# A two-part transformer on one core: the end of the expert stage re-ordered, its next pools opened earlier, and the state-space decays made a first job

## The chip, the cores and the metric

The kernel runs on 1 core of one Trainium2 chip, in one launch. The metric is the device time of that core in microseconds (us), the median of a few runs; smaller is better. The engines named below are PE (TensorE, matrix products), DVE (VectorE), ACT (ScalarE), POOL (GpSimd) and SP (SyncE, which issues most DMAs). Each works through its instructions in the order in which the program issued them.

## What is computed

512 tokens of width 1024, in fp32. Two layers run first, each of four steps; a forgetting attention, a gated MLP, an HGRN mixer and another gated MLP follow. Of a layer, this is what the change touches, in short form:

```python
x = x + merged @ w_out[i]            # the mixer; one of its four branches is bidir_ssd
x = x + expert_choice_moe(rms_norm(x, g_moe[i]), w_router[i], w_exp_gate[i], w_exp_up[i], w_exp_down[i])
ple_gate = sigmoid(rms_norm(x, g_ple[i]) @ w_ple_gate[i])
x = x + ple_gate * (p[i] @ w_ple[i])

def expert_choice_moe(h, w_router, w_gate_e, w_up_e, w_down_e):   # 16 experts, 64 tokens each
    affinity = softmax(h @ w_router)
    top_aff, idx = top_k(swapaxes(affinity, 1, 2), cap)
    xe = h[idx]
    hid = silu(xe @ w_gate_e) * (xe @ w_up_e)
    return zeros_like(h).at[idx].add((hid @ w_down_e) * top_aff)

def ssd_chunked(x, dt, a, bm, cm):                                # one direction, chunks of 128
    acs = cumsum(dt * a)                                          # within a chunk
    decay_in = exp(where(causal, acs[l] - acs[s], -inf))
    y_diag = ((cm @ bm.T) * decay_in) @ (x * dt)                  # + a state carried from chunk to chunk
```

`bidir_ssd` adds a forward and a backward pass of this over 4 heads.

## The kernel before

**Layout.** Activations stand feature-major: `x` is 8 tiles ("chunks") of 128 features x 512 tokens. Dense products split each fp32 weight into a rounded part (`ph`, a cast on ACT) and a rest (`pl`, a subtraction on DVE or POOL), and each activation chunk into two parts (both called `ach`): high part h on ACT, low part l on DVE. Each chunk then takes three 128x512 products. Expert weights are used whole, as the moving operand against 64 gathered rows.

**Expert stage** (`moe`). The 16 experts run as 8 pairs, p = 0 to 7. `gate(p)`, `up(p)` and `down(p)` each read 8 loads of 1 MB (4 per expert) and make 64 products. The program's loop over p issues: `turn` (transposes of the hidden rows), for odd p the four `gather`s of the next four experts' rows, `gate(p+1)`, for even p the `scatters` of finished pairs into `x` and `returns` (the one-hot products that bring rows back), `up(p+1)`, `down(p)`. Loads go to a ring of tiles in rotation: a main ring of 11 (`xraw`), one beside it (`xraw2`) and the shared 2 (`raw`). A load can be issued by SP only when the tile that it overwrites has been read. The first loads also borrow three tiles (`xraw3`).

**End of the stage.** After `up(7)` the main ring is closed, the pools of the next stage (`nxt`: its `ach` tiles) are opened, and a ring of 5 + 1 (`X.last`, `ring2`) with the shared 2 is opened. Then `ple_early` computes the embedding product p @ w_ple whole: a 1 MB load, two DMAs of pT, 6 casts on ACT and 6 subtractions on DVE (tiles `t2k`), and 48 products in 8 banks named `po`, each copied by ACT to `pw`. `down(6)` follows, and `down(7)` is made in two halves of output features (`half`): after half 0 all chunks get the older pairs, then chunks 0 to 3 the last pair; after half 1 chunks 4 to 7. Each `scatter(j)` sums into a bank `sm` (there are 2), DVE adds it to `x[j]` (`add_x`), and `nxt.chunk(j)` then issues for the next stage's norm: h (ACT), l (DVE), the square (ACT) and its addition (POOL or DVE). `nxt.prime(1)` loads and splits the first piece of `w_ple_gate`, at chunk 6.

**State-space branch** (`ssm`). It begins with `dt_proj`, softplus and cumulative sums (`col`, `dtv`, and `lrow`, written to memory to be read back broadcast), then convolutions (`taps`), per chunk states, and per head: `rows` (two tiles `M` of decays), `weights` (their sum, weighted by dt and multiplied by the scores `G`) and `outputs` (products into `po`). The branch is one of four jobs that the mixer's planner places beside the dense projections; it holds a cost for each instruction and a clock for each engine, and sets the order of all engines' programs when the kernel is built. Every instruction is recorded on line 196, so the trace is read by tile names.

## Time and profile before

| | |
|---|---|
| median of 3 runs | 3551.6 us (3550.32 to 3556.86) |
| the profiled execution | 3555.33 us, of which the span is 3553.5 us |
| PE busy | 3308.3 us, 93% of the span |
| DVE, ACT, POOL busy | 1708.9, 1103.9, 295.6 us |
| expert stage of layer 0, layer 1 | about 571 to 1091 us, about 1680 to 2199 us |
| mean granted PE clock | 0.977 of full speed |

The trace is one execution, its times in us from the start of the span. Launch and end, 1.83 us, lie outside the span. The clock column of a window is what the throttle granted to PE: the two levels are 1.2 and 2.4 GHz, so 1.00 means 2.4 GHz throughout, and a number between is a mix of the two. Idle time in square brackets stands ahead of the instruction in whose row it is, with what ended it.

### The profile page before, as it was taken

What the parts mean: (1) busy time and instruction counts of PE and PEld (TensorE: products, weight loads), DVE (VectorE), ACT (ScalarE), POOL (GpSimd) and SP (SyncE); (2) the same over time, 40 slices, a digit from 0 to 9 for tenths busy, and PEclk for the clock granted to TensorE, in tenths of its full rate; (3) what the DMA queues carried; (4) which work ended last, traced back from release to release, by engine and by line L of the source; (5) the groups of instructions that cost most, each with busy time, mean ns of one, the idle gap of its engine ahead of it and who ended that gap; (6) DMA issues with size and microseconds to landing.
All of it is one profiled execution on the core that took longest, in us unless ns stands there. A gap on an engine that the chain in (4) does not pass through costs nothing.

```text
span 3553.5 us, 41092 instructions
## 1 busy us (share of the span) xinstructions
PE 3308.3 (93%) x16658; PEld 2345.6 (66%) x16658; DVE 1708.9 (48%) x2914; ACT 1103.9 (31%) x1770; POOL 295.6 (8%) x176
## 2 busy tenths in 40 slices
PE   7999878998988999989999988999999999999998
PEld 6787665433336777766434434777888888878887
DVE  4565863011116546774211113654666567677555
ACT  3444322000014344322100003454434344334333
POOL 0001221000001000232000000311100000000000
PEclk9999989999999999999999999999999999999999
DMA  5242325999993332233999994222233232222222
GB/s 174 77 128 66 101 92 233 416 420 420 420 366 93 102 96 85 78 95 133 392 420 420 420 411 174 91 78 91 66 103 97 93 99 73 73 69 95 95 97 81
DMA packets 264893, 633.53 MB, mean 178 GB/s; under 512 B 20136, under 2 KB 192680, under 8 KB 215296
## 3 DMA queue, kind: packets, MB, share of 16 engines
q1 hardware_dynamic: 249136, 614.58, 46.4%
q10 hardware_dynamic: 15568, 16.32, 1.5%
q8 instruction: 131, 2.15, 0.3%
q14 instruction: 58, 0.48, 0.0%
HBM read 618.15 MB, written 4.31 MB: 175 GB/s over the span
## 4 chain that ended last, share of the span: by engine, by line
PE 42%; DMA 9%; DVE 4%; ACT 1%; issue 0%; SPq 0%; DVEq 0%; ACTq 0%
PE mm L196 36%; DMA xraw<-in_w_exp_down_dram 3%; DMA xraw<-in_w_exp_gate_dram 2%; PE po L196 2%; DMA xraw<-in_w_exp_up_dram 2%; PE sm L196 1%; PE t L196 1%; PE s L196 1%; PE a L196 1%; DVE x L196 1%; DVE pl L196 1%; DVE ach L196 1%; DMA raw<-in_w_exp_up_dram 1%; DMA raw<-in_w_exp_gate_dram 1%; DVE w L196 0%
## 5 line engine op out<-in xcount | busy, mean ns | idle before, releaser
L196 PE MATMUL mm<-ach,ph 128*128 128x512 f32 x5504 | 1748.1, 399 | 80.6 <-DVE w L196 45.7
L196 PEld LDWEIGHTS mm<-ach,ph 128*128 128x128 f32 x5504 | 1025.2, 190 | 324.8 <-issue 73.2
L196 PE MATMUL mm<-ach,pl 128*128 128x512 f32 x2752 | 1083.5, 394 | 0.5 <-DVE pl L196 0.5
L196 PEld LDWEIGHTS mm<-ach,pl 128*128 128x128 f32 x2752 | 523.3, 190 | 114.2 <-DVE pl L196 1.7
L196 PE MATMUL mm<-xraw,t2k 128*64 128x512 f32 x1776 | 461.1, 601 | 28.2 <-DMA xraw<-in_w_exp_gate_dram 21.2
L196 ACT CAST ph<-raw 128x1024 fp32r<-128x1024 f32 (+1 forms) x366 | 373.6, 1029 | 305.9 <-PE mm L196 258.9
L196 DVE TENSOR_TENSOR pl<-raw,ph 128x1024 fp32r<-128x1024 f32 (+1 forms) x317 | 389.2, 1231 | 99.8 <-ACT ph L196 97.6
L196 PEld LDWEIGHTS mm<-xraw,t2k 128*64 128x64 f32 x1776 | 146.7, 138 | 281.4 <-issue 225.9
L196 PE MATMUL mm<-xraw,hT 128*64 128x512 f32 x848 | 218.8, 599 | 26.6 <-DMA xraw<-in_w_exp_down_dram 26.6
L196 POOL TENSOR_TENSOR pl<-raw,ph 128x1024 fp32r<-128x1024 f32 x49 | 120.4, 2457 | 774.5 <-ACT ph L196 689.9
L196 DVE TENSOR_TENSOR sg<-sg,mm 128x512 f32<-128x512 f32 x32 | 22.0, 688 | 310.1 <-PE mm L196 310.1
L196 PEld LDWEIGHTS mm<-xraw,hT 128*64 128x64 f32 x848 | 68.5, 137 | 153.8 <-issue 106.4
L196 ACT ACTIVATE w<-w 128x512 f32<-128x512 f32 x130 | 80.2, 629 | 285.4 <-DVE w L196 275.0
L196 ACT ACTIVATE yy<-mm,ac 128x512 fp32r<-128x512 f32 x32 | 22.0, 687 | 419.8 <-PE mm L196 419.8
L196 DVE SCALAR_TENSOR_TENSOR yy<-mm,ac,yy 128x512 fp32r<-128x512 f32 x32 | 24.0, 751 | 248.7 <-ACT yy L196 247.7
L196 DVE SCALAR_TENSOR_TENSOR y<-u,small,y 128x512 f32<-128x512 f32 x176 | 131.8, 749 | 3.1
L196 PE MATMUL mm<-raw,t2k 128*64 128x512 f32 x272 | 124.1, 608 | 2.6 <-DMA raw<-in_w_exp_gate_dram 2.6
L196 DVE TENSOR_TENSOR x<-x,sm 128x512 f32<-128x512 f32 x80 | 54.2, 685 | 137.4 <-PE sm L196 137.4
L196 POOL TENSOR_TENSOR w<-w,w 128x512 f32<-128x512 f32 x64 | 96.1, 1513 | 272.0 <-DVE w L196 262.4
L196 DVE TENSOR_TENSOR w<-mm,R 128x512 f32<-128x512 f32 x92 | 63.0, 686 | 111.7 <-PE mm L196 104.6
L196 ACT ACTIVATE sg<-mm 128x512 f32<-128x512 f32 x32 | 19.1, 597 | 304.1 <-PE mm L196 304.1
L196 DVE TENSOR_TENSOR x<-x,mm 128x512 f32<-128x512 f32 x80 | 54.4, 684 | 122.1 <-PE mm L196 122.1
(306 smaller groups left out, 3370.0 us busy)
## 6 DMA issues: line engine op xcount, KB each, us to landing
xraw<-in_w_exp_gate_dram SPq DMA_DIRECT2D x112, 1024.0 KB, 19.9
xraw<-in_w_exp_up_dram SPq DMA_DIRECT2D x110, 1024.0 KB, 19.9
xraw<-in_w_exp_down_dram SPq DMA_DIRECT2D x106, 1024.0 KB, 19.8
raw<-in_ffn_w_up_dram SPq DMA_DIRECT2D x44, 1024.0 KB, 5.0
raw<-in_w_branch_gate_dram SPq DMA_DIRECT2D x32, 1024.0 KB, 5.3
raw<-in_w_in_dram SPq DMA_DIRECT2D x22, 1024.0 KB, 5.4
raw<-in_w_exp_down_dram SPq DMA_DIRECT2D x22, 1024.0 KB, 19.9
raw<-in_w_exp_up_dram SPq DMA_DIRECT2D x18, 1024.0 KB, 19.9
```

The source lines that it names most:

```text
L196: r = g(*a, **kw)
```

## The change

It has two parts.

**Expert stage.** (1) The 16 tiles of normalised rows (`t2k`) move to a pool of their own on the other side of memory, which is closed after the last gathers; gathered rows `xe` get 3 tiles and a shared one. (2) The rings: `ring2` is 2 instead of 1 and the last ring 6 instead of 5, and a queue of slots takes the place of the counting; `down(6)` and `down(7)` no longer use the shared `raw` tiles. (3) Closing the main ring, opening the next stage's pools and the last ring come at p = 5, after `gate(6)`. (4) `ple_early` is a generator and goes in pieces: the load of `w_ple` and the two DMAs of pT before `up(6)`; casts and subtractions after `up(6)`; 24 products after `down(5)`; 12 after `gate(7)` with its scatters and returns; 12 after `up(7)`. (5) `nxt.fetch()` issues the first two loads of `w_ple_gate` before half 1's loads, and `nxt.prime(2)` splits two pieces before half 1 is weighed. (6) The low part l and the addition of the square are issued after the next chunk's addition (`behind`), and in half 1 the odd chunks sum into a `po` bank.

**State-space branch.** `decays` (the beginning of `ssm`) is a job of its own ahead of all four, plus a small tile `ncol`. Per head, `rows` and `weights` compute the same decay weights differently: the bias of the forward decay is added on ACT, one DVE minimum joins both directions, one exponential is taken instead of two, and the weights by dt are made from two constant masks, on ACT and DVE, multiplied by `G` on POOL and by the decays on DVE.

```diff
                 eng = self.adder if j < ND - 2 else nc.vector
                 net.later(lambda q=q, t=t: eng.tensor_tensor(self.sq[q][0], self.sq[q][0], t, op=OP.add))
+
+    def fetch(self):
+
+        self.runner.fill()
+        self.runner.loads()
...
                 yield chain((lambda: N.R is not None,), self.setup_job(), self.bias_job())
+            yield chain((lambda: "setup" in self.made,), self.decays(i, dtw, xs, N, B))
             yield job(0, lambda: self.gqa(i, pj.pop("aq"), pj["akv"], rope), wait("akv", 2), lambda: "setup" in self.made)
...
             yield job(2, lambda: self.diff(i, pj.pop("cq") + pj.pop("ck"), pj.pop("cv")), wait("cv", 2), lambda: 0 in out)
-            yield job(1, lambda: self.ssm(i, dtw, xs, N, wait("x", 6), lambda: (pj.pop("z"), pj.pop("x"))), lambda: 2 in out)
+            yield job(1, lambda: self.ssm(i, B, wait("x", 6), lambda: (pj.pop("z"), pj.pop("x"))), lambda: 2 in out)
...
-    def ssm(self, i, dtw, xs, N, ready, get):
+    def decays(self, i, dtw, xs, N, B):
+
...
-        yield
+
+        ncol = self.t(wk, [128, NT, 4], F32, "ncol", 1)
+        nc.vector.tensor_scalar(ncol, col[:, 0], -1.0, None, op0=OP.mult)
+        B.dtv, B.col, B.ncol, B.wst, B.lrow = dtv, col, ncol, wst, lrow
+        yield
+
+    def ssm(self, i, B, ready, get):
+        nc, wk = self.nc, self.wk
+        dtv, col, ncol, wst, lrow = B.dtv, B.col, B.ncol, B.wst, B.lrow
...
-            for d in range(2):
-                if d:
-                    yield
-                M, msk = u.M[d], self.c("negge" if d else "negle")
-                for c in range(NT):
-                    sl = slice(c * 128, (c + 1) * 128)
-                    nc.vector.scalar_tensor_tensor(M[:, sl], M[:, sl], col[:, d, c, u.h:u.h + 1], msk, op0=OP.subtract, op1=OP.add)
-                nc.scalar.activation(M, M, AF.Exp)
...
+            f, b = u.M
+            for c in range(NT):
+                sl = slice(c * 128, (c + 1) * 128)
+                nc.scalar.activation(f[:, sl], f[:, sl], AF.Identity, bias=ncol[:, c, u.h:u.h + 1])
+            yield
+            for c in range(NT):
+                sl = slice(c * 128, (c + 1) * 128)
+                nc.vector.scalar_tensor_tensor(f[:, sl], b[:, sl], col[:, 1, c, u.h:u.h + 1], f[:, sl], op0=OP.subtract, op1=OP.min)
+            nc.scalar.activation(f, f, AF.Exp)
+
+            u.W = self.w2k()
+            for c in range(NT):
+                sl = slice(c * 128, (c + 1) * 128)
+                nc.scalar.activation(u.W[:, sl], self.c("le"), AF.Identity, scale=dtv[:, 0, c, u.h:u.h + 1])
...
-                nc.vector.tensor_scalar(u.M[0][:, sl], u.M[0][:, sl], dtv[:, 0, c, u.h:u.h + 1], None, op0=OP.mult)
-                nc.vector.scalar_tensor_tensor(u.M[0][:, sl], u.M[1][:, sl], dtv[:, 1, c, u.h:u.h + 1], u.M[0][:, sl],
-                                               op0=OP.mult, op1=OP.add)
-                if c % 2:
-                    yield
-            nc.vector.tensor_tensor(u.M[0], u.M[0], grp[g].G, op=OP.mult)
+                nc.vector.scalar_tensor_tensor(u.W[:, sl], self.c("ge"), dtv[:, 1, c, u.h:u.h + 1], u.W[:, sl], op0=OP.mult, op1=OP.add)
+            yield
+            nc.gpsimd.tensor_tensor(u.W, u.W, grp[g].G, op=OP.mult)
+            yield
+            nc.vector.tensor_tensor(u.W, u.W, u.M[0], op=OP.mult)
```

```diff
-            t2k = lambda dt=F32: self.t(wk, [128, S], dt, "t2k", 20)
+                ExitStack() as rows, self.tc.manual_schedule():
+            ph = rows.enter_context(self.work(f"rows_{X.name}", X.other))
+            t2k = lambda: self.t(ph, [128, S], F32R, "t2k", 16)
+            xe2k = lambda: self.t(wk, [128, S], F32, "xe", 3)
...
+            slots = deque()
+
+            def rotate(*kinds):
+                slots.clear()
+                for pool, tag, n in kinds:
+                    slots.extend([(pool, tag, n)] * n)
+            beside, others = (px2, "xraw2", X.ring2), (self.praw, "raw", self.RAW)
+            rotate((X.px, "xraw", X.ring), beside, others)
+            slots.rotate(-4)
+            slots.extendleft([(place.pool, "xraw3", 3)] * 3)
+            slots.extendleft([(X.px, "xraw", X.ring)] * 4)
+            once = [7]
+
...
-                x = xe[b] = t2k().rearrange("p (k c) -> p k c", k=2)
+                x = xe2k() if b < 3 else self.t(self.pn, [128, S], F32, "sqt", 1)
+                x = xe[b] = x.rearrange("p (k c) -> p k c", k=2)
...
-            def scatter(j):
-
-                ps = self.psum("sm")
+            def scatter(j, tag="sm"):
+
+                ps = self.psum(tag)
...
+                    if p == NP - 3:
+
+                        rows.close()
+                        X.close_ring()
+                        nxt.begin()
+                        nxt.ppc = nxt.pool("pcs")
+                        X.open_ring(X.last)
+                        rotate((X.px, "xraw", X.last), beside, others)
+                        early = self.ple_early(i, nxt, raw)
+                    next(early, None)
                     up(p + 1, sg)
-                if p == NP - 2:
-
-                    X.close_ring()
-                    nxt.begin()
-                    X.open_ring(X.last)
-                    for _ in self.ple_early(i, nxt, raw, t2k):
-                        pass
+                    next(early, None)
                 ys = {}
                 if p < NP - 1:
                     group.append((ys, back[p][0]))
+                    if p == NP - 2:
+                        rotate((X.px, "xraw", X.last), beside)
                     for m, py in enumerate(product(I["w_exp_down"][i], p, hT)):
                         weigh(p, m, py, ys)
+                    next(early, None)
                     continue
...
                 for m in range(2):
-                    weigh(p, m, half(I["w_exp_down"][i], p, hT, m), ys)
+                    py = half(I["w_exp_down"][i], p, hT, m)
+                    if m == 0:
+                        nxt.fetch()
+                    else:
+                        nxt.prime(2)
+                    weigh(p, m, py, ys)
                     if m == 0:
                         scatters()
                         group.append((ys, back[p][0]))
                     for j in range(4 * m, 4 * m + 4):
-                        scatter(j)
-                        if j == ND - 2:
-                            X.close_ring()
-                            nxt.prime(1)
+                        scatter(j, "po" if m and j % 2 else "sm")
+                        behind()
                         nxt.chunk(j)
-
-    def ple_early(self, i, X, raw, t2k):
+                behind()
+                self.lows = None
+                X.close_ring()
```

```diff
         nc, I = self.nc, self.I
-        ps2 = []
+        tile = lambda dt=F32: self.t(X.pa, [128, S], dt, "ach", X.ach)
         rw = raw(I["w_ple"][i], 2)
+        ps = []
         for k in range(2):
-            p = t2k()
-            nc.scalar.dma_start(p, I["pT"][i][k * 128:(k + 1) * 128])
-            h, l = t2k(F32R), t2k(F32R)
-            nc.scalar.copy(h, p)
-            nc.vector.tensor_tensor(l, p, h, op=OP.subtract)
-            ps2.append((h, l))
+            ps.append(tile())
+            nc.scalar.dma_start(ps[k], I["pT"][i][k * 128:(k + 1) * 128])
+        yield
+
+        def parts(src, view=lambda t: t):
+            h, l = tile(F32R), tile(F32R)
+            nc.scalar.copy(view(h), src)
+            nc.vector.tensor_tensor(view(l), src, view(h), op=OP.subtract)
+            return view(h), view(l)
+        ps = [parts(p) for p in ps]
+        ws = [parts(rw[:, :, b * 256:(b + 1) * 256], lambda t: t.rearrange("p (k n) -> p k n", k=2)) for b in range(4)]
         yield
         for b in range(4):
-            h, l = (t2k(F32R).rearrange("p (k n) -> p k n", k=2) for _ in range(2))
-            src = rw[:, :, b * 256:(b + 1) * 256]
-            nc.scalar.copy(h, src)
-            nc.vector.tensor_tensor(l, src, h, op=OP.subtract)
             for m in range(2):
                 sl = slice(m * 128, (m + 1) * 128)
-                ps = self.psum("po")
-                self.acc(ps, (h[:, :, sl], l[:, :, sl]), ps2)
+                bank = self.psum("po")
+                self.acc(bank, [w[:, :, sl] for w in ws[b]], ps)
                 o = self.t(X.pa, [128, S], F32, "pw", ND)
-                nc.scalar.copy(o, ps)
+                nc.scalar.copy(o, bank)
                 X.pw.append(o)
-            if b % 2:
+            if b:
                 yield
...
-        X.append(AheadMoe(net, f"e{i}", "left", "right", i, 11, 5, 1))
+        X.append(AheadMoe(net, f"e{i}", "left", "right", i, 11, 6, 2))
```

What stands where on an engine, in the programs of the two kernels:

ACT in layer 0, from the two DMAs of pT on; `t2k` and `ach` casts are those of pT and of `w_ple`. Before, this lies after `up(7)`:

```order
L196 CAST oT_6197<-po_6192 128x512
L196 CAST oT_6212<-po_6207 128x512
L196 DMA t2k_6283<-in_pT_dram 128x512
L196 CAST t2k_6285<-t2k_6283 128x512
L196 DMA t2k_6289<-in_pT_dram 128x512
L196 CAST t2k_6291<-t2k_6289 128x512
L196 CAST t2k_6295<-xraw_1216_6281 128x512
L196 COPY pw_6306<-po_6299 128x512
L196 COPY pw_6315<-po_6308 128x512
L196 CAST t2k_6317<-xraw_1216_6281 128x512
L196 COPY pw_6328<-po_6321 128x512
L196 COPY pw_6337<-po_6330 128x512
```

And now; the DMAs lie after `gate(6)`, the casts after `up(6)`, the two `yy` rows are `down(5)`'s:

```order
L196 DMA ach_5988<-in_pT_dram 128x512
L196 DMA ach_5990<-in_pT_dram 128x512
L196 CAST ach_6044<-ach_5988 128x512
L196 CAST ach_6048<-ach_5990 128x512
L196 CAST ach_6052<-xraw_5986 128x512
L196 CAST ach_6056<-xraw_5986 128x512
L196 CAST ach_6060<-xraw_5986 128x512
L196 CAST ach_6064<-xraw_5986 128x512
L196 ACTIVATE yy_6118<-mm_6068,ac_5716 128x512
L196 ACTIVATE yy_6122<-mm_6069,ac_5716 128x512
L196 COPY pw_6133<-po_6126 128x512
L196 COPY pw_6142<-po_6135 128x512
```

The six casts now stand together ahead of the first copy `pw`; before, each of the last three stood between the copies of the banks ahead of it.

DVE in layer 0, from the first addition of half 1 to the end of the stage (`x_72` to `x_75` are chunks 4 to 7, `pl` the rests of `w_ple_gate`). Before:

```order
L196 TENSOR_TENSOR x_72<-x_72,sm_6588 128x512
L196 SCALAR_TENSOR_TENSOR ach_6593<-x_72,small,ach_6592 128x512
L196 TENSOR_TENSOR x_73<-x_73,sm_6599 128x512
L196 SCALAR_TENSOR_TENSOR ach_6604<-x_73,small,ach_6603 128x512
L196 TENSOR_TENSOR x_74<-x_74,sm_6610 128x512
L196 TENSOR_TENSOR pl_6623<-raw_6618,ph_6622 128x1024
L196 TENSOR_TENSOR pl_6657<-raw_6618,ph_6656 128x1024
L196 SCALAR_TENSOR_TENSOR ach_6627<-x_74,small,ach_6626 128x512
L196 TENSOR_TENSOR sqa_6524<-sqa_6524,sqt_6630 128x512
L196 TENSOR_TENSOR x_75<-x_75,sm_6633 128x512
L196 TENSOR_TENSOR pl_6660<-raw_6620,ph_6659 128x1024
L196 SCALAR_TENSOR_TENSOR ach_6638<-x_75,small,ach_6637 128x512
```

And now:

```order
L196 TENSOR_TENSOR pl_6673<-raw_6495,ph_6672 128x1024
L196 SCALAR_TENSOR_TENSOR yy_6608<-mm_6574,ac_6305,yy_6607 128x512
L196 TENSOR_TENSOR x_72<-x_72,sm_6611 128x512
L196 SCALAR_TENSOR_TENSOR ach_6570<-x_71,small,ach_6569 128x512
L196 TENSOR_TENSOR x_73<-x_73,po_6622 128x512
L196 SCALAR_TENSOR_TENSOR ach_6618<-x_72,small,ach_6617 128x512
L196 TENSOR_TENSOR x_74<-x_74,sm_6633 128x512
L196 SCALAR_TENSOR_TENSOR ach_6629<-x_73,small,ach_6628 128x512
L196 TENSOR_TENSOR x_75<-x_75,po_6644 128x512
L196 SCALAR_TENSOR_TENSOR ach_6640<-x_74,small,ach_6639 128x512
L196 TENSOR_TENSOR sqa_6540<-sqa_6540,sqt_6642 128x512
L196 SCALAR_TENSOR_TENSOR ach_6651<-x_75,small,ach_6650 128x512
```

The `pl` rows have gone ahead of the second half (one stands first), each low part follows the next chunk's addition, and the additions read `sm` and `po` in turn.

DVE in layer 0's state-space branch, around the third head's decays (`col`, `dt`: the decays' columns and steps; `cst`: a constant mask). Before:

```order
L196 SCALAR_TENSOR_TENSOR w_3222<-w_3222,mm_3522 128x512
L196 TENSOR_TENSOR pl_3520<-raw_3404,ph_3519 128x1024
L196 SCALAR_TENSOR_TENSOR w_3479<-w_3479,col_2754,cst 128x128 x4
L196 TENSOR_SCALAR w_3386<-w_3386,dt_2664 128x128
L196 SCALAR_TENSOR_TENSOR w_3386<-w_3388,dt_2664,w_3386 128x128
```

And now:

```order
L196 TENSOR_TENSOR pl_3528<-raw_3414,ph_3527 128x1024
L196 SCALAR_TENSOR_TENSOR w_3500<-w_3502,col_585,w_3500 128x128 x4
L196 SCALAR_TENSOR_TENSOR w_3495<-cst,dt_504,w_3495 128x128 x4
L196 TENSOR_TENSOR w_3607<-mm_3559,R_266 128x512
L196 TENSOR_TENSOR pl_3611<-raw_3312,ph_3610 128x1024
L196 SCALAR_TENSOR_TENSOR w_3298<-w_3298,mm_3613 128x512
L196 TENSOR_TENSOR w_3655<-mm_3628,R_266 128x512
L196 TENSOR_TENSOR pl_3659<-raw_3567,ph_3658 128x1024
L196 TENSOR_TENSOR w_3495<-w_3495,w_3399 128x512
L196 SCALAR_TENSOR_TENSOR w_3583<-cst,dt_504,w_3583 128x128 x4
L196 TENSOR_TENSOR w_3583<-w_3583,w_3500 128x512
```

Of a head, 16 small instructions (4 for each direction's decays, and 8 of which the last two rows are the first) and one 512-wide product are now 4 + 4 small ones and one 512-wide product; the product with `G` has gone to POOL.

## Rows read from the trace of the kernel before

**Rows 1.** The page, chain of work that ended last, by engine:

```profile
PE 42%; DMA 9%; DVE 4%; ACT 1%; issue 0%; SPq 0%; DVEq 0%; ACTq 0%
```

**Rows 2.** Windows: us, engines' busy us (instructions), granted clock, DMA share, GB/s:

```profile
640.00:1000.00 360.00, 329.41 (x1586) 139.88 (x1583) 44.46 (x71) 26.07 (x44) 0.00 (x0) 0.99 1.01 420
...
1030.00:1050.00 20.00, 17.61 (x76) 7.84 (x76) 1.38 (x2) 3.96 (x7) 0.00 (x0) 1.00 0.59 224
...
1080.00:1090.00 10.00, 2.94 (x8) 1.27 (x8) 7.11 (x9) 7.00 (x10) 2.64 (x2) 0.86 0.00 0
```

**Rows 3.** Timeline of PE, 975 to 1055: start, duration, instruction [idle before]:

```profile
975.60 1.09 PE L196 MATMUL po<-cst,sg 128*128 128x128 f32 x8
...
991.97 3.65 PE L196 MATMUL mm<-xraw,t2k 128*64 128x512 f32 x14 [1.33 <-DMA xraw<-in_w_exp_gate_dram]
...
1006.68 0.64 PE L196 MATMUL mm<-xraw,t2k 128*64 128x512 f32 x1
...
1031.53 3.30 PE L196 MATMUL po<-t2k,t2k 128*128 128x512 f32 x12 [1.19 <-ACT t2k L196]
...
1039.24 3.65 PE L196 MATMUL mm<-raw,hT 128*64 128x512 f32 x16
...
1053.13 1.09 PE L196 MATMUL po<-cst,sg 128*128 128x128 f32 x8
```

**Rows 4.** Timeline of PE, half 1 and the next stage's first products:

```profile
1072.72 7.09 PE L196 MATMUL mm<-xraw,hT 128*64 128x512 f32 x32
...
1091.68 1.19 PE L196 MATMUL mm<-ach,ph 128*128 128x512 f32 x2 [6.12 <-DVE x L196]
```

**Rows 5.** The same of layer 1:

```profile
2199.74 1.19 PE L196 MATMUL mm<-ach,ph 128*128 128x512 f32 x2 [5.80 <-DVE x L196]
```

**Rows 6.** Timeline of DVE at the end of layer 0's expert stage:

```profile
1080.60 0.75 DVE L196 SCALAR_TENSOR_TENSOR yy<-mm,ac,yy 128x512 fp32r<-128x512 f32 x1 [2.77 <-ACT yy L196]
...
1087.02 2.65 DVE L196 TENSOR_TENSOR pl<-raw,ph 128x1024 fp32r<-128x1024 f32 x2
...
1090.86 0.67 DVE L196 TENSOR_TENSOR x<-x,sm 128x512 f32<-128x512 f32 x1
```

**Rows 7.** Groups by shape, PE, 1091.6 to 1097.8: busy, mean ns | idle before:

```profile
L196 PE MATMUL mm<-ach,ph 128*128 128x512 f32 x10 | 5.2, 622 | 6.1 <-DVE x L196 6.1
```

**Rows 8.** The same, PE, 1110 to 1140:

```profile
L196 PE MATMUL mm<-ach,ph 128*128 128x512 f32 x89 | 27.4, 389 | 0.0
```

**Rows 9.** Timeline of SP's DMA issues:

```profile
912.06 0.33 SPq L196 DMA_DIRECT2D xraw<-in_w_exp_gate_dram  x1
...
1010.36 0.33 SPq L196 DMA_DIRECT2D xraw<-in_w_ple_dram  x1
```

**Rows 10.** Groups by shape, 336 to 486 (state-space branch, layer 0), DVE and POOL:

```profile
L196 DVE SCALAR_TENSOR_TENSOR w<-w,col,cst 128x128 f32<-128x128 f32 x32 | 20.4, 698 | 4.1 <-DMA w<-lrow 4.1
...
L196 DVE TENSOR_SCALAR w<-w,dt 128x128 f32<-128x128 f32 x16 | 8.7, 544 | 0.0
...
L196 POOL TENSOR_TENSOR w<-w,w 128x512 f32<-128x512 f32 x21 | 31.1, 1496 | 78.6 <-DVE w L196 78.6
L196 POOL TENSOR_TENSOR pl<-raw,ph 128x1024 fp32r<-128x1024 f32 x5 | 12.1, 2412 | 10.3 <-ACT ph L196 10.3
```

**Rows 11.** Timeline of DVE, then of POOL, in the last two heads:

```profile
458.97 2.38 DVE L196 TENSOR_SCALAR w<-w,dt 128x128 f32<-128x128 f32 x1
...
467.68 0.28 DVE L196 TENSOR_SCALAR w<-w,dt 128x128 f32<-128x128 f32 x1
467.99 0.35 DVE L196 SCALAR_TENSOR_TENSOR w<-w,dt,w 128x128 f32<-128x128 f32 x1
...
458.86 2.41 POOL L196 TENSOR_TENSOR pl<-raw,ph 128x1024 fp32r<-128x1024 f32 x1
```

**Rows 12.** Windows as in Rows 2, over the state-space branch:

```profile
460.00:486.00 26.00, 12.38 (x59) 10.88 (x60) 16.07 (x32) 4.48 (x7) 3.75 (x3) 0.68 0.12 42
336.00:486.00 150.00, 117.40 (x528) 94.99 (x527) 114.62 (x181) 45.98 (x67) 42.95 (x26) 0.91 0.30 92
```

More of the change, by code (lines that the diff above doesn't have):

```diff
@@ L789, in mixer @@
         pj = {}
-        merged, ms, gt = {}, [], {}
+        merged, ms, gt, B = {}, [], {}, Box()
         out = {}
@@ L1406, in outputs @@
                 o = grp[g].py[r * 64:(r + 1) * 64, sl]
-                self.mm(o, xt[g][:, c, r * 64:(r + 1) * 64], u.M[0][:, sl], start=True, stop=False)
+                self.mm(o, xt[g][:, c, r * 64:(r + 1) * 64], u.W[:, sl], start=True, stop=False)
                 if c > 0:
@@ L1744, in moe @@
             up(0, sg, rv=first[1])
+            early = iter(())
             for p in range(NP):
```

34 lines of the change are left out of this document (16 added, 18 removed).

## The prediction

> **What bounds the kernel now.** I began with the chain of work that ended last: PE is the largest part of it, DMA 9%, DVE 4% [rows 1]. So a saving counts where PE waits, or where DMA or DVE stands in the chain. The windows show where that is. From 640 to 1000, inside the first layer's expert stage, the DMA engines are full (share 1.01) while PE is busy 329 of 360 us [rows 2]: weights arrive at their limit, and PE time there is not scarce. From 1030 to 1050 the share is only 0.59, with PE nearly full [rows 2]: there the end of the stage has become PE's. From 1080 to 1090 nothing moves and PE is busy 2.94 of 10 us [rows 2]: that is DVE's tail. The timeline of PE gives the same in single steps: before 1000, 16 products of 3.65 us wait 1.33 us for their two loads [rows 3], thus 4.98 us for two loads or 2.49 for one; then the stage goes by PE's own work, and at 1091.68 PE has stood 6.12 us for DVE [rows 4]. Layer 1 shows the like wait of 5.80 us [rows 5], so I cost one layer and double it. The second place is the state-space branch, 336 to 486: PE 117.4, DVE 114.6, POOL 43.0 busy of 150 us [rows 12]; both wait for each other, and the clock is granted at 0.91.
>
> **The end of the expert stage up to its last half.** Before, `gate(7)` ends at 991.97 + 3.65 = 995.6; up(7) begins at 1006.68, 11.1 later; `down(6)` takes 1053.13 − 1039.24 = 13.9, and `up(7)`, of as many products, the same, so that it ends at 1020.6; the embedding product fills 1020.6 to 1039.24 = 18.6 us [rows 3]. Its 48 products at 3.30 per 12 are 13.2 [rows 3]; 5.4 are waits for casts and subtractions, as the 1.19 ahead of the last two thirds [rows 3].
>
> After, step by step. (a) The load of `w_ple` (2.49) and the pT DMAs (half its bytes, 1.2) go ahead of `down(5)`'s loads; one more slot in the early ring lets one load (2.49) start earlier; and the 7th load of `up(6)` has to await pT's landing, 0 to 2 us of empty queue. Together +1.2 to +3.2; I take 3.2, the dear end, because the pause falls where DMA is the limit. SP itself, held at the closing of the ring from its issue at 912.06 on as it is now before the load at 1010.36 [rows 9], has some eight loads outstanding then, 8 × 2.49 = 20 us of work, so that the hold alone costs nothing if it ends by 932. `down(5)`, which ends at 975.6 [rows 3], then ends at 978.8. (b) 24 products: 6.6, `turn` 1.1 [rows 3], `gate(7)` without waits 4 × 3.65 = 14.6: 1001.1. Its last loads were there at 991.97, and are now at 995.2 at the latest, 2 us before their use: PE sets the pace here, and half of the embedding product has gone into time in which PE waited for loads. (c) + 11.1 + 3.3 (12 products) + 13.9 (`up(7)`) + 3.3 + 13.9 (`down(6)`) = 1046.6. (d) From `turn` to half 1 it was 1072.72 − 1053.13 = 19.6 [rows 3, 4]; with l behind the next addition, DVE's 0.75 [rows 6] no longer stands between additions for chunks 0 and 1: less 1.5. Half 1 begins at 1064.7 and ends 7.1 later, 1071.8, against 1079.8 [rows 4]: 8.0 us earlier. The loads for the last half I work out to land at about 1067, by adding the bytes left at the full rate to a queue that stands still some 6 us near 1025, where 8 slots wait for `up(7)` to read; the second pair is wanted at 64.7 + 3.6 = 1068.3. The margin is thin, so I take **7**. Ends: 3, if loads come 4 late; 10, if (a) costs nothing.
>
> **The tail.** From the end of half 1 to the next stage's first product: 1091.68 − 1079.8 = 11.9 us [rows 4]. In it DVE does two subtractions of the next weights (2.65) ahead of the last low parts, and the first product had to wait until chunk 7 was added at 1090.86 + 0.67 [rows 6]. Now three subtractions run under half 1, since their loads are issued before that half's, and the first product's bank is free after chunk 6. The sum: second part of yy done at 1080.60 + 0.75, 1.5 after the half [rows 6]; 0.5 for products; three additions at 0.67 and two low parts at 0.75 = 3.5 [rows 6]; 5.5, and up to 0.9 more where the third subtraction runs over. Gain 11.9 − 6.2 = **5.7**; ends 4.5 and 6.4. The first 15 products there took 622 ns [rows 7], where at the full clock it is 389 [rows 8]: 15 × 0.233 = 3.5, after a window granted 0.86 [rows 2]. With half the idle time I take **1.5**, ends 0 and 3. The two loads ahead of half 1's cost 5 us of DMA that had to move anyway.
>
> Per layer 7 + 5.7 + 1.5 = 14.2.
>
> **The state-space branch.** Per head DVE loses 4 fused instructions (0.35 each undisturbed, taken from the like one) and 4 scalings (0.28) [rows 11]: 2.5 us, 10.1 a layer; by the group means of 698 and 544 ns it would be 20 [rows 10]. Those means are long because POOL holds DVE: a 0.28 us scaling took 2.38 beside a 2.41 us POOL subtraction [rows 11]. POOL gains 4 products of 1.50 us [rows 10], 6.0 a layer if DVE stands still for each. 10.1 − 6.0 = 4.1, of which not all is on the path (PE waits 32.6 of 150): **+3** a layer. Ends: −5.6, if each product also stands behind a POOL subtraction of 2.41 us [rows 10] and DVE with it (2.5 − 1.5 − 2.4 = −1.4 a head); +9, if POOL never meets DVE. ACT's added instructions, eight a head on a quarter of the width, have no row; they lie between 0.28 and 0.75 (DVE's small and full width [rows 6, 11]), at most 24 us on an engine that is busy 46 of 150 [rows 12], so I cost them at nothing. `decays` first: the convolutions still wait for the x projections, and PE's order from there is the same; nothing gained, ±2 a layer for the attention jobs that it pushes back. The pool of rows, tile `ncol` and the gathers' tiles keep their counts: nothing.
>
> The Trainium skill says the same of POOL ("SBUF — State Buffer", section Who interferes with whom): a DVE instruction with two SBUF inputs contends with a GpSimd instruction that reads SBUF, and the one that comes second blocks until the first is done. The 2.38 us agree. It speaks against the product on POOL: as a rule for each of the four it makes 4.1 a layer at best, and B below where products queue.
>
> **Sum.** 2 × (14.2 + 3) = 34.4. The profiled execution had 3555.33, 3.7 over the median: 3520.9 for it, and 3551.6 − 34.4 = **3517** for the median.
>
> **Rivals.**
> A: the loads are late at the end. The last ring has 8 slots, each freed by PE; a second pause like the one near 1025 makes half 1 wait. For it: the share of 0.59 shows that the queue already runs dry there [rows 2]. Then the 7 is gone: 2 × (7.2 + 3) = 20.4, 3531.
> B: POOL's products queue behind subtractions and hold DVE, as in [rows 11]: −5.6 a layer, 2 × (14.2 − 5.6) = 17.2, 3534. Against: POOL mostly waits for DVE (78.6 us [rows 10]) and is busy 43 of 150 [rows 12].
> C: every term at its good end, 2 × (10 + 6.4 + 3 + 9) = 56.8, 3495.
> D: the tail isn't shortened, since the first products meet low parts that come as late as before: 2 × (7 + 3) = 20, 3532. Against: the order of the additions.
> E: slower. In the branch PE's clock falls. It was granted 0.68 at the branch's end, where PE was busy 12.4 of 26 us waiting for the last heads [rows 12]. The last head's chain now goes DVE, POOL, DVE for what DVE did alone; if that holds PE at every head, 117.4 us of work at 0.75 instead of 0.91 take 25.0 more: 2 × (25.0 − 14.2) = 21.6, 3573. It outweighs the rest from 14.2 on, that is below a clock of 0.81. Against: the chain is 1.4 + 1.5 + 0.7 where it was 2.5 + 0.7, nearly as long.
>
> **Chances.** Forecast 0.48, A 0.17, B 0.13, C 0.12, D 0.05, E 0.05. A measurement of this kernel can tell some 0.2%, 7 us, from no change. Faster by more than that: all but E and the far sides of A, B and D, 0.90; within it 0.05; slower 0.05. The range 3497 to 3540 holds A, B, D and half of C; beyond it lie E, the other half of C and A with B together (3548).
>
> **What would show it.** After `down(5)` 24 products of the embedding with no wait ahead, and `gate(7)` without its 1.33; no block of 18.6 us ahead of `down(6)`; half 1 ending near 1072 relative to the stage's begin; first products some 6 us later, with a wait of 3 to 4 in place of 6.12; no more DVE instructions of over 1.2 us in the branch than before. Against me: a wait for `in_w_exp_down` ahead of either half (A), DVE instructions of 1.3 us and more in the new groups (B), a granted clock under 0.85 over the branch (E). The forecast is wrong above all if `down(6)` and the halves wait for loads.

## The result, and the profile after

The changed kernel took 3512.1 us, median of 4 runs (3502.07 to 3514.31), against 3554.2 for the kernel before (4 runs, 3550.32 to 3557.66): a ratio of 0.9876, 95% interval 0.9853 to 0.9899, or 42 us less (36 to 52). 3517 was forecast, with a range of 3497 to 3540. The profiled run took 3513.49 with a span of 3511.7; PE is busy 94% of it.

The table cuts both spans at the same instructions of PE's timeline (us; L0 and L1 are the two layers).

| stretch | before | after | change | forecast |
|---|---|---|---|---|
| start to first gather of the expert stage, L0 | 595.2 | 586.2 | −9.0 | −3 |
| gather to end of `down(5)`, L0 | 380.4 | 384.2 | +3.8 | +3.2 |
| to start of `down(6)`, L0 | 63.6 | 52.3 | −11.3 | −9.7 |
| to end of half 1, L0 | 40.6 | 41.1 | +0.6 | −1.5 |
| to first product of the next stage, L0 | 11.9 | 7.75 | −4.1 | −5.7 |
| from there to first gather, L1 | 610.4 | 592.2 | −18.2 | −4.5 |
| gather to end of half 1, L1 | 485.9 | 475.2 | −10.7 | −7 |
| to first product of the next stage, L1 | 11.85 | 7.75 | −4.1 | −5.7 |
| from there to PE's end | 1344.8 | 1356.1 | +11.2 | −1.5 |

The forecast column is the prediction's terms by stretch; its three steps for L0's stage make the 8.0 worked out there, of which 7 were taken, as for L1.

Timeline of PE after the change, end of layer 0's expert stage (start, duration, instruction, [idle before]); it answers to [rows 3, 4]:

```profile
966.77 3.65 PE L196 MATMUL mm<-xraw,hT 128*64 128x512 f32 x14 [1.33 <-DMA xraw<-in_w_exp_down_dram]
970.35 5.74 PE L196 MATMUL po<-ach,ach 128*128 128x512 f32 x24
...
987.70 3.60 PE L196 MATMUL mm<-xraw,sqt 128*64 128x512 f32 x16
...
1002.95 2.98 PE L196 MATMUL po<-ach,ach 128*128 128x512 f32 x12 [0.51 <-DVE ac L196]
...
1019.75 3.01 PE L196 MATMUL po<-ach,ach 128*128 128x512 f32 x12
1022.69 13.95 PE L196 MATMUL mm<-xraw,hT 128*64 128x512 f32 x64
...
1037.99 4.51 PE L196 MATMUL mm<-xraw,hT 128*64 128x512 f32 x18 [0.33 <-ACT hT L196]
1043.56 3.65 PE L196 MATMUL mm<-xraw,hT 128*64 128x512 f32 x14 [1.06 <-DMA xraw<-in_w_exp_down_dram]
...
1056.74 7.09 PE L196 MATMUL mm<-xraw,hT 128*64 128x512 f32 x32
1065.51 0.50 PE L196 MATMUL sm<-oT,yy 128*128 128x512 f32 x1 [1.69 <-ACT yy L196]
1067.47 0.80 PE L196 MATMUL sm<-oT,yy 128*128 128x512 f32 x1 [1.46 <-DVE yy L196]
...
1071.57 1.22 PE L196 MATMUL mm<-ach,ph 128*128 128x512 f32 x2 [0.74 <-DVE x L196]
```

Read it against the steps. 24 products of the embedding stand behind `down(5)` with nothing ahead of them. `gate(7)`'s last products wait for no load. The block of 18.6 us ahead of `down(6)` is gone. But the first half of `down(7)` now waits 1.06 us for a load and takes 9.2 us, where half 1 takes 7.1; and the products behind half 1 wait 1.69 and 1.46 us for `yy`. The wait of 6.12 us ahead of the next stage's first product is now 0.74, where the prediction had 3 to 4: the waiting has gone to `yy`.

Two of the signs against the forecast did appear, without the price put on them: the wait for `in_w_exp_down` (A's sign), ahead of half 0, and DVE instructions of 1.3 us and more in a new group (B's sign): of the sixteen minima in the group `w<-w,col,w` below, six take 1.35 to 1.40 us. Before, eleven of 32 decays did. DVE instructions of over 1.2 us in the branch fell from 36 to 28.

Groups by shape over the state-space branch of layer 0 after the change, 327 to 477 (busy us, mean ns of one | idle before), which answer to [rows 10], and its window, which answers to [rows 12]:

```profile
L196 DVE SCALAR_TENSOR_TENSOR w<-w,col,w 128x128 f32<-128x128 f32 x16 | 10.7, 728 | 2.4 <-ACT w L196 2.4
...
L196 DVE SCALAR_TENSOR_TENSOR w<-cst,dt,w 128x128 f32<-128x128 f32 x16 | 4.5, 341 | 0.0
...
L196 ACT ACTIVATE w<-w,ncol 128x128 f32<-128x128 f32 x16 | 5.1, 391 | 2.1 <-DMA w<-lrow 2.1
L196 ACT ACTIVATE w<-cst,dt 128x128 f32<-128x128 f32 x16 | 5.1, 388 | 0.0
```

```profile
327.00:477.00 150.00, 122.83 (x546) 100.38 (x545) 97.45 (x152) 54.24 (x97) 48.98 (x30) 0.90 0.31 96
```

The sixteen fused additions of before, which [rows 10] leaves out:

```profile
L196 DVE SCALAR_TENSOR_TENSOR w<-w,dt,w 128x128 f32<-128x128 f32 x16 | 7.4, 465 | 0.6
```

With the two groups for decays and scalings of [rows 10] they took 36.5 us of DVE; 15.2 are left. ACT's added 32 instructions cost 10.2 us.

### The profile page after: what moved, and what is told of

The parts are those of the page before. It is cut to its first block, busy times and chain, and to the rows that moved or that the text cites. A ratio compares the mean times of both kernels' runs of the same rounds, so it can differ in the third digit from the quotient of the medians.

```text
span 3511.7 us, 41101 instructions
## 1 busy us (share of the span) xinstructions
PE 3311.0 (94%) x16658; PEld 2356.6 (67%) x16658; DVE 1682.0 (48%) x2852; ACT 1118.4 (32%) x1826; POOL 309.7 (9%) x184
## 4 chain that ended last, share of the span: by engine, by line
PE 72%; DMA 15%; DVE 9%; ACT 2%; issue 2%; POOL 1%; SPq 0%; DVEq 0%; ACTq 0%; POOLq 0%
PE mm L196 58%; DMA xraw<-in_w_exp_down_dram 6%; PE po L196 5%; PE t L196 4%; DMA xraw<-in_w_exp_gate_dram 3%; PE sm L196 3%; DMA xraw<-in_w_exp_up_dram 3%; DVE w L196 3%; DVE pl L196 2%; PE s L196 2%; DVE x L196 1%; DVE ach L196 1%; PE a L196 1%; ACT ph L196 1%; DMA ach<-in_pT_dram 1%
## 5 line engine op out<-in xcount | busy, mean ns | idle before, releaser
L196 PE MATMUL mm<-xraw,xe 128*64 128x512 f32 x1312 | 330.9, 599 | 17.7 <-DMA xraw<-in_w_exp_gate_dram 10.4
L196 PE MATMUL mm<-xraw,hT 128*64 128x512 f32 x928 | 228.5, 595 | 22.3 <-DMA xraw<-in_w_exp_down_dram 21.5
L196 PEld LDWEIGHTS mm<-xraw,xe 128*64 128x64 f32 x1312 | 104.7, 138 | 202.5 <-issue 166.4
L196 POOL TENSOR_TENSOR w<-w,w 128x512 f32<-128x512 f32 x72 | 110.4, 1545 | 250.8 <-DVE w L196 243.8
L196 PE MATMUL mm<-xraw,sqt 128*64 128x512 f32 x448 | 118.3, 606 | 9.3 <-DMA xraw<-in_w_exp_gate_dram 6.6
## 6 DMA issues: line engine op xcount, KB each, us to landing
xraw<-in_w_exp_down_dram SPq DMA_DIRECT2D x116, 1024.0 KB, 18.7
```

The source lines that it names most:

```text
L196: r = g(*a, **kw)
```

## The experiments

Each was timed beside the kernel before on the same chip; its median there was 3557.6 in the first and third group of runs and 3562.1 in the second.

**1 to 3: the parts alone.** `e1_expert_part` is the kernel before with the change to the expert stage and its fetching, `e2_state_space_part` with the change to the state-space branch. `e3_decays_first` has of the latter only the job moved ahead, with the arithmetic as before:

```diff
+            yield chain((lambda: "setup" in self.made,), self.decays(i, dtw, xs, N, B))
             yield job(0, lambda: self.gqa(...
...
-            yield job(1, lambda: self.ssm(i, dtw, xs, N, wait("x", 6), ...
+            yield job(1, lambda: self.ssm(i, B, wait("x", 6), ...
```

> The expert-stage part of the change alone, on the kernel before; the state-space branch as before. If the two parts of the change are independent, the trace should show layer 0's last half ending 7 us earlier relative to the stage's first gather and the next stage's first product another 4 us earlier, the like in layer 1, 25 to 28 us in all by the traces of the two kernels: about 3527 us. Rival: part of the 19 us that the second mixer gains comes from this part (the stage ahead of it ends otherwise): then 3515 to 3520.

> The state-space part alone (decays as a first job, and the decay weights rewritten), expert stage as before. By the prediction's term 2 x 3 us: 3548. By the two traces, where the mixers are 9.0 and about 18 us shorter: 3527. Rival: the mixers' gain needs the expert part: 3540 or more.

> Only the order of jobs: the decays are a first job of their own, the weights computed as before. The prediction held this for worth nothing, plus or minus 2 us a layer. The two traces have the first convolution 4 us earlier in layer 0 and 10 us earlier in layer 1 (relative to the stage before), which would be 3540; the rest of the mixers' gain, 5 and 8 us, would then be the rewriting.

Measured: e1 3537.8, ratio 0.9941 (0.9927 to 0.9956), 20 us less; e2 3535.7, 0.9935 (0.992 to 0.995), 22 less; e3 3553.8 over 10 runs, 0.9992 (0.9978 to 1.0005), nothing that can be told. The two parts add up to the whole. In e1's trace the stretch from gather to the next stage's first product is 11.0 (L0) and 14.8 us (L1) shorter, as expected, with tails of 7.45 and 7.74, while the stretches ahead of the two first gathers change by +3.3 and −1.8; that its time stays 11 us above the 3527 expected is in good part stretches that it leaves as they were (6 us longer together, the last one alone 4.6). In e2's the tails are 11.87 and 11.84 as before, and the stretches ahead of the two gathers are 10.4 and 14.4 us shorter. So the gain ahead of the expert stage belongs to the state-space part, and within it, by e2 against e3, to the rewritten arithmetic: 18 us by the medians, 9 a layer. That the early job alone does nothing is not shown: PE's idle time (under 9) is 7 us less in e3.

**4: is POOL's product the price that was put on it?** The product goes back to DVE:

```diff
-            nc.gpsimd.tensor_tensor(u.W, u.W, grp[g].G, op=OP.mult)
+            nc.vector.tensor_tensor(u.W, u.W, grp[g].G, op=OP.mult)
```

> The changed kernel with the product by G on DVE instead of POOL. If a POOL product holds DVE for its 1.5 us as the prediction costed it, DVE gains 1.5 and pays 0.7 for each of 8: 0 to 6 us faster, 3506 to 3512. Rival: POOL's products run where DVE has no work that matters, and the added 0.7 us stands in the chain of each head: 3 to 8 us slower, 3515 to 3520.

3507.1 (0.9852, 0.9833 to 0.9872): not told apart from the changed kernel, and within the 3506 to 3512 expected if POOL does hold DVE, so the time does not decide. The traces do, by the views under 9. If each of the eight products held DVE for its 1.5 us, DVE would be busy 6.4 us less here (eight times 1.5 less 0.7); it is busy 707.9 us, against 697.3 and, in e12, 702.1. PE's idle time is 96.3 (98.9 in e8, which has the same edit), against 100.5 and 100.0. So DVE is not held as I charged, and moving the products off POOL again gains PE 1 to 4 us in both layers together, where the charge would make 6.4.

**5: what is the place of the embedding products worth?** All 48 stand behind `up(7)` again; casts and loads stay early:

```diff
-                    next(early, None)
+                    if p == NP - 3:
+                        next(early, None)
                     up(p + 1, sg)
-                    next(early, None)
+                    for _ in range(1 if p == NP - 3 else 4):
+                        if p >= NP - 3:
+                            next(early, None)
```

> The changed kernel with the 48 products of the embedding in one block after up(7), all else (early load, early casts, early pools, late low parts) as changed. If the 24 products after down(5) are free because gate(7) would else wait for its loads, gate(7) ends where it ends now (991.2 in layer 0) and the block costs 12 x 0.5 more after it: half 1 ends some 6 us later in each layer, about 3524. Rival: the gain comes from the casts that no longer stand between products, and the place of the products is worth nothing: within 3 us of 3512.

3511.0 (0.9868, 0.985 to 0.9887), not told apart from the changed kernel by its time. PE's timeline of it:

```profile
980.20 3.22 PE L196 MATMUL mm<-xraw,xe 128*64 128x512 f32 x13 [1.33 <-DMA xraw<-in_w_exp_gate_dram]
985.18 3.65 PE L196 MATMUL mm<-xraw,sqt 128*64 128x512 f32 x14 [1.33 <-DMA xraw<-in_w_exp_gate_dram]
...
1015.47 11.19 PE L196 MATMUL po<-ach,ach 128*128 128x512 f32 x48
...
1041.89 7.09 PE L196 MATMUL mm<-xraw,hT 128*64 128x512 f32 x32 [0.33 <-ACT hT L196]
```

`gate(7)`'s waits are back and `down(6)` starts 5.4 us later than in the changed kernel, counted from `down(5)` (57.7 against 52.3), but then the first half has its weights: from half 0 to half 1 it is 16.6 us instead of 18.7. The block takes 11.19 us, where [rows 3] had 18.6 with its waits for casts. In all, gather to the next stage's first product takes 488.1 and 487.6 us, where the changed kernel has 485.4 and 482.9 (485.4 and 484.0 in e12). So filling `gate(7)`'s load waits gains 2.7 to 4.6 us a layer, between the 6 expected and the nothing of the rival, since loads wait for PE a few us later; the larger part of the stage's gain is kept without it.

**6 and 7: two details of the tail.** e6 adds the low parts at once; e7 splits the next stage's weights behind half 1's additions instead of ahead of them:

```diff
-                self.lows = lows = []
+                lows = []
```

> The changed kernel, but each chunk's low part and square addition issued at once, ahead of the next chunk's addition, as before the change. By the prediction's terms half 1 begins 1.5 us later after half 0, and the next stage's first product 2 to 3 us later after half 1 (each addition waits for ACT's high part of the chunk ahead): 4 us a layer. Rival: the additions are paced by PE anyway, and nothing moves.

```diff
-                    else:
-                        nxt.prime(2)
                     weigh(p, m, py, ys)
...
+                        if j == ND - 2:
+                            nxt.prime(2)
                         nxt.chunk(j)
```

> The changed kernel, but the next weights split at chunk 6, as before the change, and not ahead of the second half's weighing; their loads still issued early. In the changed kernel the weighing after half 1 waits for three casts and subtractions (1.69 and 1.46 us ahead of PE's scatters); here it should start 2 us earlier, and the first product then wait for subtractions behind chunk 6: first product 7 to 9 us after half 1 instead of 7.75. If the early splitting is what shortened the tail, it is 10 us or more.

One run each, 3513.8 and 3513.2, so read by their traces. PE's timeline at the next stage's first product, of e6 and then of e7:

```profile
1073.82 1.22 PE L196 MATMUL mm<-ach,ph 128*128 128x512 f32 x2 [3.68 <-DVE x L196]
```

```profile
1067.60 0.51 PE L196 MATMUL sm<-oT,yy 128*128 128x512 f32 x1 [0.79 <-ACT yy L196]
...
1074.32 1.22 PE L196 MATMUL mm<-ach,ph 128*128 128x512 f32 x2 [4.04 <-ACT ph L196]
```

In e6, half 0 to half 1 takes 20.3 (18.7 in the changed kernel), the 1.5 that I gave to the later low parts, and its tail is 8.8 instead of 7.75: 2.6 us in all, for 4 expected. In e7 `yy` comes earlier but the first product then waits for its casts: 7.50 behind half 1, as good as 7.75. Splitting early is worth nothing by itself here: what `yy` loses, the casts gain. So of the 4.1 us by which the tail is shorter the late low parts carry 1.0. The rest, 3 us, stays with the early loads and the second bank for the sums, which no run took apart.

**8: more work off POOL.** On top of e4, the sums of squares for chunks 1 to 3 that the next stage needs go to DVE, so that ACT's squares do not wait for POOL:

```diff
-                eng = self.adder if j < ND - 2 else nc.vector
+                late = j < ND // 2 and self.name[0] == "p"
+                eng = self.adder if j < ND - 2 and not late else nc.vector
```

> A version meant to beat both: product by G on DVE (as in e4), and in the stage after the experts the squares of chunks 1 to 3 added on DVE instead of POOL. In the changed kernel ACT waits 0.95 and 0.78 us for POOL to free the one tile of squares, and so the three casts end 1 us after half 1. Without these waits the tail from half 1 to the first product should be 6 us instead of 7.75 in each layer: 3 to 4 us faster than e4, about 3503. Rival: the additions on DVE lie in the chain of chunk 4 and give it back.

3502.3 (3500.09 to 3504.28), 0.9835 (0.9821 to 0.985): lower than the kernel before, and the lowest of all. The tail is 7.13, not the 6 expected: 0.6 of 7.75. ACT's waits for POOL of 0.95 and 0.78 (below) become 0.41 and 0.54 for DVE, yet the casts still come ahead of `yy`, with waits of 1.00 and 1.22 for it. The tail explains 1.2 us of two layers. The 3503 expected were met for another reason as well: the records grant PE the clock's lower level for 134 us in e8's trace and for 154 in e12's, which is worth more than the 5.7 us between these two executions. That e8 is faster than e4 is not shown: they ran on different chips, at 0.9835 and 0.9852.

**9: is it DVE's busy time?** The kernel before with its 16 scalings a layer on ACT:

```diff
-                nc.vector.tensor_scalar(u.M[0][:, sl], u.M[0][:, sl], dtv[...], None, op0=OP.mult)
+                nc.scalar.activation(u.M[0][:, sl], u.M[0][:, sl], AF.Identity, scale=dtv[...])
```

> The kernel before, with only the scaling by dt of each head's decays (16 DVE instructions of a quarter width a layer) moved to ACT. It prices what the rewriting took from DVE. If they cost what they take undisturbed (0.28 us), each mixer gains at most 4.5 us; by the group's mean of 0.54 us, which holds the time in which POOL blocks them, up to 8.7. In two layers 3549 by the first, 3540 by the second; 0 to 3 us in all if DVE is not what the branch waits for.

3554.9 over 10 runs, 0.999 (0.9979 to 1.0001): nothing. The two stretches ahead of the first gathers of the expert stages, summed (us, busy PE, PEld, DVE, ACT, POOL, then their means), of the kernel before, the changed kernel, e3, e4 and e9:

```profile
sum 1205.61, PE 1085.50 PEld 857.27 DVE 723.47 ACT 450.87 POOL 207.18; mean PE 542.75 PEld 428.63 DVE 361.74 ACT 225.43 POOL 103.59
```

```profile
sum 1178.39, PE 1077.93 PEld 854.15 DVE 697.32 ACT 467.14 POOL 222.35; mean PE 538.97 PEld 427.08 DVE 348.66 ACT 233.57 POOL 111.18
```

```profile
sum 1200.70, PE 1087.28 PEld 861.52 DVE 721.88 ACT 451.44 POOL 205.34; mean PE 543.64 PEld 430.76 DVE 360.94 ACT 225.72 POOL 102.67
```

```profile
sum 1178.20, PE 1081.88 PEld 857.12 DVE 707.90 ACT 467.35 POOL 212.64; mean PE 540.94 PEld 428.56 DVE 353.95 ACT 233.68 POOL 106.32
```

```profile
sum 1206.45, PE 1088.28 PEld 861.38 DVE 709.13 ACT 460.03 POOL 206.16; mean PE 544.14 PEld 430.69 DVE 354.56 ACT 230.02 POOL 103.08
```

The sum less PE's busy time is PE's idle time: 120.1, 100.5, 113.4, 96.3 and 118.2 us. DVE is busy 708 us in e4 and 709 in e9, but PE is idle for 96 us in the one and 118 in the other. PE's waits over the branch of layer 0 (us in total, times, longest), in windows of 150 us, of before, after and e9:

```profile
PE mm L196 <- DVE w L196: 16.6, 7, 5.6
...
PE po L196 <- DVE w L196: 8.7, 4, 4.5
```

```profile
PE mm L196 <- DVE w L196: 10.5, 5, 3.2
...
PE po L196 <- DVE w L196: 9.0, 2, 4.8
```

```profile
PE mm L196 <- DVE w L196: 16.6, 7, 5.3
...
PE po L196 <- DVE w L196: 9.8, 3, 5.5
```

What falls in the changed kernel, and not in e9, is PE's wait ahead of projections (`mm`): 16.6 to 10.5 us, the longest from 5.6 to 3.2. In e4 it is 10.5 too. In layer 1 the two waits part less clearly: 16.0 and 6.1 before, 13.2 and 3.1 after, 13.5 and 5.7 in e9. So DVE's sum is not what counts; that it is how much stands in its queue ahead of what PE waits for is my reading of these waits. Which part of the rewriting does it is open. e9 leaves in place the eight decay instructions per head that became four, but also the two exponentials on ACT that became one and weights by dt that wait for the decays; no run changed one of these alone.

**10: the decays as a late job** in the changed kernel, behind `diff`:

```diff
-            yield chain((lambda: "setup" in self.made,), self.decays(i, dtw, xs, N, B))
             yield job(0, ...
...
+            yield chain((lambda: 0 in out,), self.decays(i, dtw, xs, N, B))
             yield job(1, ...
```

> The changed kernel with the decays still a job of their own, but placed behind the third branch's job, once the first is done, about where they ran before the change. e3 made the early place alone worth 0 to 5 us. If that holds beside the rewriting too, this is 0 to 5 us slower than the changed kernel (3512 to 3517); if the rewriting needs the early decays, 10 us or more.

3513.5 (0.9867, 0.9842 to 0.9892): as the changed kernel. The view of 9 for it:

```profile
sum 1181.03, PE 1081.01 PEld 853.53 DVE 706.08 ACT 466.54 POOL 225.21; mean PE 540.50 PEld 426.77 DVE 353.04 ACT 233.27 POOL 112.60
```

PE is idle for 100.0 us, as in the changed kernel (100.5): by these traces the early place is worth nothing beside the rewriting, and the rewriting without it takes away the same 20 us.

**11: the slots of the ring.** The changed kernel with the slot counts of before:

```diff
-        X.append(AheadMoe(net, f"e{i}", "left", "right", i, 11, 6, 2))
+        X.append(AheadMoe(net, f"e{i}", "left", "right", i, 11, 5, 1))
```

> The changed kernel with the rings as before the change (one tile less in the early ring, 5 + 1 instead of 6 + 2 at the end). Rival A of the prediction: loads late at the end. In the changed kernel half 0 waits 1.06 us for a load. With 6 slots instead of 8 the halves should wait 3 to 8 us in each layer; if loads have slack there, nothing moves.

3525.3 in one run. Gather to `down(5)`'s end takes 390.4 and 389.4 us instead of 384.2 and 381.3. Windows of the changed kernel, then window and PE's timeline of e11:

```profile
910.00:930.00 20.00, 20.00 (x116) 10.42 (x117) 2.77 (x4) 0.97 (x2) 0.00 (x0) 1.00 0.98 398
```

```profile
910.00:930.00 20.00, 19.93 (x110) 9.78 (x109) 2.31 (x4) 1.19 (x2) 0.00 (x0) 1.00 0.78 313
...
934.44 5.35 PE L196 MATMUL mm<-xraw,xe 128*64 128x512 f32 x16 [4.50 <-DMA xraw<-in_w_exp_up_dram]
```

The shortage of loads that I looked for at the stage's end stands where the early ring is handed over to the last: with one slot fewer in the last ring and one in the ring beside it, the DMA share there is 0.78 and PE waits 4.50 us for `up`'s weights. Half 0's load waits are 0.30 and 1.46 in it, half 1 has none: the 3 to 8 expected at the halves did not come. From gather to the end of half 1 e11 takes 485.4 and 485.2 us, as the kernel before (484.6, 485.8). So by this run the two slots carry the whole gain of the stage up to there; it does not tell them apart.

**12: the changed kernel again.**

> The changed kernel once more, beside the others, for a second trace: which stretches repeat, and how far the granted clock moves the stages that the change leaves as they were. Stretches between fixed points should repeat within 1 us where the granted clock is the same; the stages behind the second layer, 4 to 7 us longer than before the change in the first trace at a lower granted clock, should come nearer to those of before.

3510.8 (0.9864, 0.9842 to 0.9886). Layer 0's stretches repeat within 0.2 us of the table, layer 1's within 1.4. The last one does not: 1349.3 us, 6.8 less than in the first trace, and so nearer to that of before, as expected.

## Why the prediction held, point by point

**The end of the stage: right in sum, less so in its parts.** Forecast 7 a layer, measured 7.0 and 10.7. Layer 1's figure holds 1.7 of clock: half 1 took 8.78 there before, at a granted clock of 0.81, and 7.09 after, for the same products. Gather to end of half 1 takes 484.2 to 488.5 us in the other traces with the stage of before (e2, e3, e9) and 475.1 to 478.1 in others with the new one (e1, e4, e10, e12), so that 7 is at the low end. The parts came differently: (a) 3.8 for 3.2; (b) and (c) 11.3 for 9.7, most of it because the 48 products take 5.7 + 3.0 + 3.0 = 11.7 us, and not 13.2; (d) 0.6 lost where 1.5 was to be gained. The low parts do bring their 1.5 (e6), but half 0 takes 2.1 us longer for want of a load. My margin of 1.3 us was worked out for half 1, which waits for none; half 0's loads I had not followed. That is rival A in small, one half earlier. The 3.8 of (a) holds only with the two added slots, of which I had priced the one in the early ring, at 2.49 us: without both it is 6 to 8 more a layer, and nothing is left of the gain (e11). My reason for (b) was half right: by e5 the place of the products is worth 2.7 to 4.6 us a layer, and the rest of the gain does not need it.

**The tail: too large.** 4.1 measured, 5.7 forecast. The step that failed is "second part of yy done 1.5 after the half". ACT and DVE, then DVE, in the changed kernel:

```profile
1059.40 0.63 ACT L196 ACTIVATE sqt<-x 128x512 f32<-128x512 f32 x1 [0.95 <-POOL sqa L196]
1061.42 0.63 ACT L196 ACTIVATE sqt<-x 128x512 f32<-128x512 f32 x1 [0.78 <-POOL sqa L196]
1061.95 2.92 ACT L196 CAST ph<-raw 128x1024 fp32r<-128x1024 f32 x3
1064.78 0.68 ACT L196 ACTIVATE yy<-mm,ac 128x512 fp32r<-128x512 f32 x1
...
1063.01 3.74 DVE L196 TENSOR_TENSOR pl<-raw,ph 128x1024 fp32r<-128x1024 f32 x3 [3.10 <-ACT ph L196]
1066.68 0.74 DVE L196 SCALAR_TENSOR_TENSOR yy<-mm,ac,yy 128x512 fp32r<-128x512 f32 x1
```

Half 1 ends at 1063.83. The squares wait for POOL, so the three casts begin at 1061.95 and end a microsecond after the half; the subtractions that need them hold DVE to 1066.7, and `yy` is complete at 1067.42, 3.6 after the half. I had costed the subtractions and not what releases them. From there the sum holds: 4.1 to the first product, where I had 0.5 + 3.5 = 4.0.

**The clock behind the tail: not there.** The fifteenth product begins 5.95 and 4.98 us behind the first before, 5.52 and 5.57 after: 0.4 gained in layer 0 and 0.6 lost in layer 1, for 1.5. In the 12.5 us behind the first product the records grant the lower level for 5.8 and 3.6 us before, 4.8 and 4.9 after. With half the idle time I had assumed half the loss; the shorter wait did not bring it.

**The state-space branch: a third of what came.** +3 forecast, 9.0 in layer 0; of layer 1's 18.2 between the stages 10.7 is PE's idle time less (45.9 to 35.2), and the rest is PE's busy time (564.5 to 556.9), as the lower level of the clock was granted for 47.2 us there before and 32.4 after. In idle time alone the two layers gain 9.0 and 10.7. Three steps were wrong. The removed work was priced at 10.1, undisturbed, when DVE's trace shows 21.3 less; the 20 by the group means, which I had set aside, was right. The product on POOL was priced at 6.0 a layer; less the 2.8 that the four take on DVE that is 3.2, and e4 and e8 show 0.5 to 2. And the whole was priced by DVE's busy time, of which 14.3 us can go with 1.9 less of PE's idle time (e9). The Trainium skill ("SBUF — State Buffer", Who interferes with whom) has a DVE instruction with two SBUF inputs contend with a GpSimd one that reads SBUF. The minima, which read two tiles, agree: four of them, alone and then beside three products on POOL, in the changed kernel:

```profile
412.46 1.14 DVE L196 SCALAR_TENSOR_TENSOR w<-w,col,w 128x128 f32<-128x128 f32 x4 [2.37 <-ACT w L196]
...
439.63 4.22 DVE L196 SCALAR_TENSOR_TENSOR w<-w,col,w 128x128 f32<-128x128 f32 x4
...
438.66 4.79 POOL L196 TENSOR_TENSOR w<-w,w 128x512 f32<-128x512 f32 x3 [8.79 <-DVE w L196]
```

The 2.38 us that the prediction set beside that rule show a block too, but of a scaling, which reads one tile and a column of factors. Yet the rule tells how long an instruction takes, not what it costs: rival B, built on it, did not come about. The costs put at nothing were right: early decays (e10) and ACT's additions, 10.2 us against my bound of 24.

**Behind the expert stages: a loss that I had not in the sum.** The code there is unchanged. Windows over it, of before, after and e12:

```profile
2200.00:3544.00 1344.00, 1328.14 (x6931) 1102.29 (x6931) 819.68 (x1355) 547.11 (x842) 75.24 (x43) 0.99 0.27 85
```

```profile
2147.00:3502.00 1355.00, 1338.42 (x6930) 1111.43 (x6930) 822.53 (x1358) 549.36 (x845) 76.51 (x45) 0.99 0.26 84
```

```profile
2147.00:3496.00 1349.00, 1332.29 (x6932) 1105.85 (x6932) 822.36 (x1358) 549.42 (x845) 76.88 (x45) 0.99 0.26 84
```

The same number of products, to within a record or two, keeps PE busy for 1328, 1338 and 1332 us. The records grant the clock's lower level, 1.2 GHz, for 16.2, 37.5 and 23.2 us of these windows, and half of the difference is about what the busy time gains. So 10 us of the 11.2 are clock, and two traces of one kernel differ by 6.8. The change has no part in it that can be told: in the four traces with the expert stage of before (before, e2, e3, e9) this last stretch takes 1344.8 to 1353.2 us, in the ten with the new one 1346.1 to 1356.1. The forecast came within 5 us in part by luck. The traces gain 41.8 where it had 34.4, and the kernel before, timed again, took 3554.2, where the sum began from 3551.6. And the 34.4 is as near as that because errors of opposite sign met: by the table 19.7 us more gain in the two stretches with the branch and 3.6 more in the two stages, 3.2 less in the tails, and 12.7 less at the end. E did not come: the branch's clock was 0.90, where it was 0.91 before.

## What to carry to other kernels

What an instruction costs on an engine with a queue in order is the wait of those behind it: before pricing removed work by its busy time, look who stands behind it and who waits for that one. Where products are moved into a wait for loads, ask which loads then come late; here some 3 to 5 us of 7 to 11 hung on the place, and the rest on what was done ahead. Where one ring of buffers hands over to the next, count the slots across the handover: here the shortage showed there, and not where the last loads are used. And read a small gain in PE's idle time and by stretch: the total also holds the clock, which differs from run to run.

## What the hardware showed that I had not expected

The granted clock fell to 1.2 GHz for 16 to 37 us in the unchanged last 1344 us, with PE busy 99% of them, and for different lengths in two traces of the same kernel. On this kernel that is worth 3 to 11 us, as much as the gain of a whole term, so a difference of that size should be looked for in the stretch that was changed before it is believed. The same wait can have either outcome. PE, of before, after and e12, at one place of the last stage:

```profile
3174.33 0.38 PE L196 MATMUL sm<-cst,sqa 128*128 128x1 f32 x2 [2.84 <-DVE sqa L196]
```

```profile
3128.42 0.59 PE L196 MATMUL sm<-cst,sqa 128*128 128x1 f32 x2 [2.85 <-DVE sqa L196]
```

```profile
3122.92 0.38 PE L196 MATMUL sm<-cst,sqa 128*128 128x1 f32 x2 [2.86 <-DVE sqa L196]
```

The lower level was granted for none, 10.2 and 6.8 us from about there on. And products of 128x512 on POOL, 1465 ns each by their group, cost little beside a DVE that is busy 97 of 150 us: 1 to 4 us of PE's idle time for eight of them, by e4 and e8.
